# A list schedule that puts an unread product ahead of a ready TensorE operation, by the work over the last clock window

## The chip, the cores and the metric

The kernel runs on one core of one Trainium2 chip. The metric is the device time of that core in microseconds (us), as the median of several executions; lower is better. The core has five engines that the text names as the profile does: PE (TensorE; its weight loads are PEld), DVE (VectorE), ACT (ScalarE), POOL (GpSimd) and SP (SyncE, which here only issues transfers). PE's clock is granted in steps: the profile gives it for every stretch of time as a share of full speed, and here it shows 1.00 or 0.50.

## What is computed

Four layers over one sequence of 512 tokens with 1024 features, each a mixer and then a gated feed-forward block, with a residual sum after both. The four mixers differ. Cut to what matters here:

```python
for i in range(DEPTH):                        # DEPTH = 4
    t = i % 4
    hn = rmsnorm(h, norm_mix[i])
    m = [rwkv7_mix, swa_sink_mix, sgu_chunk_mix, gla_mix][t](hn, ...)
    h = h + m
    h = h + swiglu(rmsnorm(h, norm_ffn[i]), ffn_w_in[i], ffn_w_out[i])
return rmsnorm(h, norm_final)

# rwkv7_mix, one step of its recurrence per token, 16 heads of 64 x 64 states
sa = einsum('bhvk,bhk->bhv', state, kk_t)
state = state * d_t - sa * (kk_t * a_t) + v_t * k_t
y_t = einsum('bhvk,bhk->bhv', state, r_t)
# ... then a norm per head, a gate, and  @ w_o

# swa_sink_mix, 16 query heads on 2 key heads, window of 128 tokens
s = einsum(q, k) / 8, masked;  p = exp(s - max) / (sum + exp(sink - max))
o = einsum(p, v);  return o @ w_o + b_o
```

## The kernel before

**An order that a program writes.** The kernel's code doesn't issue instructions as it runs. Each call on an engine makes an `Op` with its data dependences and an estimated cost (`record`, `price`), and `Program.run` then issues all of them in the order of a list schedule: it keeps an estimated time `now` for each engine, looks at the operations whose inputs are issued within a window of 700, works out for each when it could start (`s`), and takes the one that starts first. All engines run their own queues in that order, so an order that the schedule chose for PE is kept on the chip even where another operation would be ready earlier. Every instruction made in this way carries one line number in the profile, L233 (L234 in the changed kernel); groups are told apart by their tiles.

**Unread products.** The schedule also fills waits of PE. `keep_warm` is called when the operation that was chosen for PE has to wait for its inputs; if the estimated wait is at least `GAP` (450 ns), it issues products of the 128x128 identity with itself (`product`, L448; L478 in the changed kernel) into a PSUM bank that nobody reads, as many as fit until 150 ns before the operation can start. A product is estimated at 224 ns, or 448 ns where the schedule takes the clock for halved. It does so where the columns that it has booked for the tick before (a tick is 10240/3 ns, on a fixed grid; `count` books them) are fewer than `BUSY` = 3350, and it then doubles the estimated cost of any PE operation as well. In the profile one unread product is two records, since a 4-byte product is made in two passes there: `ps<-ident 128*128`.

**The stages that the text speaks of.** All times are of the profiled execution.

- *The RWKV mixer* runs from the start to about 500 us, in four sub-blocks of four heads each. For each: features are prepared (`rwkv_prepare`, whose 512-wide working tiles are called `et`), products of pairs of tokens are made (`rwkv_products`, into `pr`), a triangular matrix is inverted by blocks (`rwkv_inverse`: 16 small products at a time with ACT or DVE between, tiles `mt`, result `iv`), it is applied (`rwkv_direct`), and a chain of eight steps goes over the tokens (`rwkv_chain`): a product gives `x`, ACT copies it into `vu`, a product with `tok` makes the next state, DVE scales it into `st`, and `st` goes into the next step's products. The chain's outer products (`wu` with `iv`, `vu` with `pr`) hang beside it, and `rwkv_out` turns its results (`out`) round with the identity. When the last sub-block's chain ends, the output projection is left: `rwkv_out_proj`, 288 products `et,rk` (moving `et`, stationary `rk`; six of the eight head pairs, 256 columns wide).
- *The attention mixer* (`swa`, about 860 to 1010 us): four query projections for the first key head (`project`: 24 products of 512 columns each, rows `slot,whi` and `slot,wlo`), its scores (`slot 128x256` and `slot 128x128`), a softmax over DVE, ACT and POOL, turning the weights round (`ident,slot`), and the products with the values (`slot 64x512`). The second key head's four projections are independent of the first one's softmax, and so is the output projection's (`whi,slot`, `gemm_tok`) first half of the second one's. I call the two key heads group 1 and group 2.
- Behind 1010 us come the feed-forward block, the other two mixers and their blocks, in which PE hardly waits.

Of the kernel before, what the change touches and what calls it, by code (L numbers as in the profile page):

```python
# [17 lines left out]
P = 128  # L18
# [19 lines left out]
class View:  # L38
# [3 lines left out]
    def __init__(self, buf, dims, p0, lo, steps):  # L42
        self.buf, self.dims, self.p0, self.lo, self.steps = buf, dims, p0, lo, steps
# [146 lines left out]
class Program:  # L190
# [3 lines left out]

    WINDOW, SLACK, SEM = 700, 200.0, 100.0
    FREE, GAP, TAIL, TURN = 4, 450.0, 150.0, 92.0
    TICK, BUSY = 10240 / 3, 3350.0

    def __init__(self, tc):
        self.tc, self.ops, self.last = tc, [], None  # L200
        nc = tc.nc
        self.tensor, self.vector, self.scalar = Engine(self, "PE", nc.tensor), Engine(self, "DVE", nc.vector), Engine(self, "ACT", nc.scalar)
        self.gpsimd, self.sync = Engine(self, "POOL", nc.gpsimd), Engine(self, "SP", nc.sync)
        self.cold, self.warm, self.fills, self.form = 0.0, None, 0, (P, P, 0)

    def pool(self, name, bufs, **kw):
        return Pool(self, name, bufs, kw)
# [80 lines left out]
    def run(self):  # L288
# [9 lines left out]
        now = {e: 0.0 for e in ("PE", "DVE", "ACT", "POOL", "SP", "")}  # L298
        dma, table, work = 0.0, None, {}
# [4 lines left out]
        while order < n:  # L304
            while head < n and ops[head].done:
                head += 1
            new = min(n, head + self.WINDOW)
            for op in ops[limit:new]:
                if op.wait == 0:
                    bisect.insort(avail[op.eng], (op.i, op))  # L310
            limit = max(limit, new)
            best = None
            for e, lst in avail.items():
                cand, floor = None, None
                for i, op in lst:
                    s = max(now[e], op.ready)
                    ok = True
                    for b in op.bufs:
                        if b.held:
                            continue  # L320
                        sl = b.pool.slots[b.name]
                        if not sl.may(b, head) or b.psum and b.span[0] > head and len(sl.free) <= self.FREE and not self.soon(b, head):
                            ok = False
                            break
                        s = max(s, min(sl.free) + self.SEM)
                    if not ok:
                        continue
                    if op.table and op.table != table and not (table and op.table in ALSO.get(table, ())):
                        s += 1300.0
                    if floor is None or s < floor - self.SLACK:  # L330
                        if floor is None or s < floor:
                            floor = s
                        cand = (s, i, op)
                    elif s < floor:
                        floor = s
                    if floor <= now[e]:
                        break
                if cand:

                    if best is None or cand[0] < best[0]:  # L340
                        best = cand + (e,)
            if best is None:
                raise RuntimeError("no instruction can go on at %d of %d: %s" % (order, n, [(e, len(l)) for e, l in avail.items()]))
            s, i, op, e = best
            if e == "PE" and self.warm and op.ready > 0.0:
                now["PE"] = self.keep_warm(now["PE"], s, work)
                if now["PE"] > s:
                    continue
            avail[e].remove((i, op))
            if op.table and op.table != table and not (table and op.table in ALSO.get(table, ())):  # L350
                table = op.table
            cost = op.cost
            if e == "PE":
                if op.form[:2] != self.form[:2]:
                    cost += self.TURN
                elif op.form[0] == 64 and op.form[2] != self.form[2]:
                    cost *= 0.56
                self.form = op.form
                tick = int(s // self.TICK)
                if work.get(tick - 1, 0.0) < self.BUSY:  # L360
                    self.cold += cost
                    cost *= 2
                self.count(work, self.TICK, s, cost, op.columns)
            end = s + cost
            now[e] = end
            fin = end + op.lat
            if op.lat == 2000.0:
                dma = max(dma, s + 1100.0) + max(450.0, op.columns / 360.0)
                fin = dma + 1500.0
            op.end = end  # L370
            for b in op.bufs:
                if not b.held:
                    b.pool.slots[b.name].take(b, head)
            op.call()
            op.done = True
            order += 1
            for b in op.bufs:
                b.till = max(b.till, fin if op.lat == 2000.0 else end + 60.0)
                b.left -= 1
                if b.left == 0:  # L380
                    b.pool.slots[b.name].give(b, head)
            for o in op.outs:
                raw = o.deps[op]
                if o.eng == e and e == "PE" or o.eng == "":
                    t = end
                elif o.eng == e:
                    t = (fin if raw else end) if op.lat != 2000.0 else fin
                else:
                    t = fin if raw else (end + self.SEM if op.lat != 2000.0 else fin)
                o.ready = max(o.ready, t)  # L390
                o.wait -= 1
                if o.wait == 0 and o.i < limit:
                    bisect.insort(avail[o.eng], (o.i, o))
        self.time = max(now.values())

    def keep_warm(self, now, s, work):
# [7 lines left out]
        while True:  # L404
# [7 lines left out]
            t += c  # L412
            now = t

    def count(self, work, span, t, cost, columns):
        n = int(t // span)
        part = min(1.0, ((n + 1) * span - t) / cost)
        work[n] = work.get(n, 0.0) + columns * part
        work[n + 1] = work.get(n + 1, 0.0) + columns * (1.0 - part)
# [1397 lines left out]
```

## Time and profile before

| | us |
|---|---|
| median of 3 runs | 2604.38 |
| the runs | 2601.57, 2606.51, 2604.38 |
| the profiled execution, its own time | 2596.65 |
| its span in the trace | 2595.0 |
| PE busy in it | 2517.9 (97%) |
| unread products | 190 (380 records) |
| granted PE clock, mean | 0.994 |

The profiled execution was 7.7 us faster than the median. The page gives the span and the busy time of each engine; beside it the prediction uses the view of windows (for a stretch of time each engine's busy time and instruction count, the clock granted to PE, the share of the DMA engines), the timeline of one engine (in square brackets the idle time before an instruction, and the operation whose end released it), the groups of instructions by line and form, and the view of waits. The window rows have these columns: from:to in us, length, then busy time and count of PE, PEld, DVE, ACT and POOL, PE clock, DMA share, GB/s.

### The profile page before, as it was taken

The numbers are of one execution on the slowest core, as the hardware profiler recorded it, in microseconds if no ns is written. First come the engines' busy times: TensorE is split into PE (matmuls) and PEld (weight loads), VectorE is DVE, ScalarE is ACT, GpSimd is POOL, SyncE is SP. The second block draws the span as 40 slices with busy tenths as digits, with TensorE's granted clock in tenths as the row PEclk, the third lists the DMA queues.
The fourth block names the chain that finished last, engine by engine and source line by source line (L and its number), as shares of the span: only waits on it lengthen the run. The fifth ranks groups of instructions, "written<-read, shape, count | busy, mean of one in ns | idle before, by whom it ended". The sixth has DMA issues, their size and how long they took to land.

```text
span 2595.0 us, 37573 instructions
## 1 busy us (share of the span) xinstructions
PE 2517.9 (97%) x14378; PEld 2052.6 (79%) x14378; DVE 1802.4 (69%) x2804; ACT 1314.1 (51%) x2156; POOL 377.6 (15%) x521
## 2 busy tenths in 40 slices
PE   9999898999999989999999999999999999999998
PEld 8577777997888756988787888888878777888886
DVE  8685875487778863787776655577868634577868
ACT  4544454465646455656464333565556523565555
POOL 1000111022112232121221000012111000121111
PEclk9999999999999999999999999999999999999999
DMA  3220001489898412898985232389887221489885
GB/s 128 62 75 10 10 4 59 120 195 225 214 225 176 129 49 49 179 211 225 213 218 146 90 98 83 82 216 228 208 213 187 84 81 57 98 219 226 221 199 117
DMA packets 126004, 365.20 MB, mean 141 GB/s; under 512 B 13296, under 2 KB 19952, under 8 KB 125824
## 3 DMA queue, kind: packets, MB, share of 16 engines
q0 software_dynamic: 41472, 138.43, 29.8%
q1 hardware_dynamic: 84352, 224.37, 26.9%
q8 instruction: 113, 1.85, 0.3%
q14 instruction: 67, 0.55, 0.1%
HBM read 358.29 MB, written 2.10 MB: 139 GB/s over the span
## 4 chain that ended last, share of the span: by engine, by line
PE 47%; DMA 5%; issue 5%; DVE 4%; ACT 3%; POOL 0%; SPq 0%; ACTq 0%; POOLq 0%; DVEq 0%
PE ps L233 47%; DMA wraw<-ffn_w_b 3%; DVE slot L233 2%; ACT slot L233 2%; DMA wraw<-ffn_o_a 2%; DVE wlo L233 1%; ACT whi L233 1%; DMA wraw<-ffn_w_a 1%; DVE h L233 0%; POOL wraw L233 0%; DVE mx L233 0%; DMA slot<-slot 0%; SPq L233 0%; DVE left L233 0%; ACT left L233 0%
## 5 line engine op out<-in xcount | busy, mean ns | idle before, releaser
L233 PE MATMUL ps<-whi,slot 128*128 128x512 f32 (+1 forms) x5072 | 1557.7, 384 | 17.8 <-DVE slot L233 9.3
L233 PEld LDWEIGHTS ps<-whi,slot 128*128 128x128 f32 x5072 | 943.7, 188 | 199.5 <-issue 21.4
L233 DVE TENSOR_TENSOR wlo<-wraw,whi 128x1024 fp32r<-128x1024 f32 (+2 forms) x628 | 720.2, 1153 | 398.8 <-ACT whi L233 396.4
L233 ACT CAST whi<-wraw 128x1024 fp32r<-128x1024 f32 (+3 forms) x632 | 625.1, 993 | 732.2 <-PE ps L233 554.7
L233 PE MATMUL ps<-wlo,slot 128*128 128x512 f32 (+1 forms) x2536 | 969.1, 383 | 1.9 <-DVE wlo L233 1.7
L233 PEld LDWEIGHTS ps<-wlo,slot 128*128 128x128 f32 x2536 | 476.9, 188 | 86.1 <-DVE wlo L233 6.2
L233 PE MATMUL ps<-slot,whi 128*128 128x512 f32 (+2 forms) x864 | 275.8, 397 | 0.1
L233 DVE TENSOR_TENSOR slot<-ps,slot 128x512 f32<-128x512 f32 (+2 forms) x287 | 155.0, 566 | 91.0 <-PE ps L233 61.7
L233 PEld LDWEIGHTS ps<-slot,whi 128*128 128x128 f32 (+2 forms) x864 | 157.2, 185 | 48.3 <-issue 6.6
L233 POOL DMA_DIRECT2D wraw<-ffn_w_a x128 | 109.1, 853 | 512.5 <-DVE wlo L233 375.7
L233 PE MATMUL ps<-slot,wlo 128*128 128x512 f32 (+2 forms) x432 | 169.5, 393 | 0.8 <-DVE wlo L233 0.8
L233 POOL DMA_DIRECT2D wraw<-ffn_w_b x64 | 54.7, 859 | 772.7 <-DMA wraw<-ffn_w_b 517.8
L233 DVE TENSOR_TENSOR slot<-left,slot 128x512 fp32r<-128x512 f32 (+1 forms) x214 | 137.5, 661 | 34.3 <-ACT slot L233 28.8
L233 DVE TENSOR_TENSOR h<-h,ps 128x512 f32<-128x512 f32 x192 | 127.1, 683 | 29.8 <-PE ps L233 28.4
L233 ACT CAST slot<-left 128x512 fp32r<-128x512 f32 (+1 forms) x214 | 123.8, 598 | 34.3 <-PE ps L233 26.4
L233 PEld LDWEIGHTS ps<-ident,slot 128*128 128x128 f32 (+1 forms) x676 | 69.2, 141 | 41.9 <-POOL slot L233 14.4
L233 ACT COPY slot<-ps 128x512 f32<-128x512 f32 (+1 forms) x137 | 75.2, 563 | 50.8 <-PE ps L233 49.2
L233 PE MATMUL ps<-ident,slot 128*128 128x128 f32 (+1 forms) x676 | 89.4, 268 | 11.4 <-POOL slot L233 9.0
L233 PEld LDWEIGHTS ps<-slot,wlo 128*128 128x128 f32 (+2 forms) x432 | 79.6, 184 | 21.3 <-issue 3.3
L233 POOL DMA_DIRECT2D wraw<-ffn_o_a x64 | 54.5, 852 | 278.6 <-DVE wlo L233 204.9
L233 ACT COPY left<-ps 128x512 f32<-128x512 f32 x100 | 50.5, 555 | 54.7 <-PE ps L233 54.7
L233 DVE TENSOR_TENSOR slot<-slot 128x512 fp32r<-128x512 f32 (+9 forms) x93 | 62.0, 672 | 15.8 <-ACT slot L233 14.6
(278 smaller groups left out, 2267.3 us busy)
## 6 DMA issues: line engine op xcount, KB each, us to landing
wraw<-ffn_w_a SPq DMA_DIRECT2D x128, 512.0 KB, 6.5
wraw<-ffn_w_a POOLq DMA_DIRECT2D x128, 512.0 KB, 6.1
wraw<-ffn_o_a SPq DMA_DIRECT2D x64, 512.0 KB, 5.0
wraw<-ffn_o_a POOLq DMA_DIRECT2D x64, 512.0 KB, 8.0
wraw<-ffn_w_b SPq DMA_DIRECT2D x64, 384.0 KB, 3.3
wraw<-ffn_w_b POOLq DMA_DIRECT2D x64, 384.0 KB, 6.2
wraw<-ffn_o_b SPq DMA_DIRECT2D x16, 512.0 KB, 4.3
wraw<-ffn_o_b POOLq DMA_DIRECT2D x16, 512.0 KB, 7.7
```

Of the source, the lines that this page charges most:

```text
L233: op = self.add(eng.name, lambda: getattr(eng.target, what)(*map(real, args), **{k: real(a) for k, a in kw.items()}), *self.price(eng.name ...
```

## The change

A method `ahead_of_cold` is called for a PE operation that could start without a wait worth filling. It adds up the columns that PE was given over the last tick's length, up to the end of that operation (a sliding sum over `recent`, which `count` now fills, and not the fixed grid). If the sum is `DENSE` = 3550 or more, the operation is issued, as before, and a flag `armed` is set that is never cleared. If it is less and the flag is set, one unread product is issued ahead of the operation, PE's estimated time moves on by its cost, and the schedule chooses anew among all engines and operations.

```diff
-    TICK, BUSY = 10240 / 3, 3350.0
+    TICK, BUSY, DENSE = 10240 / 3, 3350.0, 3550.0
...
+        self.recent, self.armed = [], False
...
             if e == "PE" and self.warm and op.ready > 0.0:
                 now["PE"] = self.keep_warm(now["PE"], s, work)
-                if now["PE"] > s:
+                if now["PE"] > s or self.ahead_of_cold(now, s, op, work):
                     continue
...
+    def ahead_of_cold(self, now, s, op, work):
+        pool, call, first = self.warm
+        free = pool.slots["ps"].free
+        t, end = max(s, now["PE"]), s + op.cost
+        if not first.done or not free or min(free) + self.SEM > t:
+            return False
+        sum_ = op.columns
+        for b, e, c in reversed(self.recent):
+            if e <= end - self.TICK:
+                break
+            sum_ += c * (e - max(b, end - self.TICK)) / (e - b)
+        if sum_ >= self.DENSE:
+            self.armed = True
+            return False
+        if not self.armed:
+            return False
+        cost = 224.0 if work.get(int(t // self.TICK) - 1, 0.0) >= self.BUSY else 448.0
+        call()
+        self.fills += 1
+        self.form = P, P, 0
+        self.count(work, self.TICK, t, cost, 512.0)
+        now["PE"] = t + cost
+        return True
+
     def count(self, work, span, t, cost, columns):
+        self.recent.append((t, t + cost, columns))
+        if len(self.recent) > 400:
+            del self.recent[:200]
```

Since an added product moves PE's estimated time, it moves the choice of everything behind it, and the order changes in more places than the products stand. There are 280 unread products now, 90 more: 77 net in the RWKV mixer and 13 in the attention mixer. From about 1010 us on PE's order is the same. Three places on PE matter to the prediction.

The first is the last sub-block's inverse (PE, after the wait at 407 us; `mt`, `pr`, `iv` as above, `wu,iv` and `vu,pr` are outer products of chains that run beside it). Before:

```order
L233 MATMUL ps<-wu,iv 64x64 x5
L233 MATMUL ps<-mt 64x64 x16
L233 MATMUL ps<-wu,iv 64x64 x7
L233 MATMUL ps<-ident,mt 64x64 x16
L233 MATMUL ps<-vu,pr 64x64 x3
L233 MATMUL ps<-mt,pr 64x64 x16
L233 MATMUL ps<-vu,pr 64x64
L233 MATMUL ps<-wu,iv 64x64 x2
```

The same place now:

```order
L478 MATMUL ps<-ident 128x128 x2
L234 MATMUL ps<-mt 64x64 x16
L478 MATMUL ps<-ident 128x128 x4
L234 MATMUL ps<-ident,mt 64x64 x16
L478 MATMUL ps<-ident 128x128 x3
L234 MATMUL ps<-mt,pr 64x64 x16
L478 MATMUL ps<-ident 128x128 x4
```

The outer products that stood between the steps have gone behind the inverse, and unread products stand in their place, ahead of each step.

The second is the end of the last chain and the output projection (PE, about 455 to 475 us; `tg,g` is the gate). Before:

```order
L233 MATMUL ps<-vu,tok 128x128 x2
L233 MATMUL ps<-vu,pr 64x64 x4
L233 MATMUL ps<-ident,out 128x128
L233 MATMUL ps<-tg,g_3900 128x256
L233 MATMUL ps<-st_1420,qk 128x128 x2
L233 MATMUL ps<-tg,g_3900 128x256
L233 MATMUL ps<-et,rk 128x256
L233 MATMUL ps<-vu,pr 64x64 x4
L233 MATMUL ps<-et,rk 128x256 x80
L233 MATMUL ps<-ident,out 128x128 x4
L233 MATMUL ps<-et,rk 128x256 x207
```

Now:

```order
L234 MATMUL ps<-vu,tok 128x128 x2
L234 MATMUL ps<-vu,pr 64x64 x4
L234 MATMUL ps<-et,rk 128x256 x5
L234 MATMUL ps<-ident,out 128x128 x4
L234 MATMUL ps<-st_1420,qk 128x128 x2
L234 MATMUL ps<-et,rk 128x256 x9
L234 MATMUL ps<-vu,pr 64x64 x4
L234 MATMUL ps<-et,rk 128x256
L234 MATMUL ps<-ident,out 128x128 x4
L234 MATMUL ps<-tg,g_3985 128x256 x2
L234 MATMUL ps<-et,rk 128x256 x75
L234 MATMUL ps<-ident,out 128x128 x4
```

Of the 288 products `et,rk`, 32 now stand between the steps of the last chain, the first of them right after its first step. The rest, 75 and 181, follow as before.

The third is the wait for group 1's softmax (PE, about 902 to 909 us; with buffer numbers, since the rows read alike without them: `whi_8992` and `wlo_9004` are the weights of one query projection, `ident,slot` is the first turning round). Before:

```order
L233 MATMUL ps_9206<-slot_8970,slot_9166 128x256
L233 MATMUL ps_9218<-slot_8697,whi_8992 128x512
L233 MATMUL ps_9218<-slot_8708,whi_8992 128x512
L233 MATMUL ps_9218<-slot_8697,wlo_9004 128x512
...
L233 MATMUL ps_9218<-slot_8716,whi_8992 128x512
L233 MATMUL ps_9218<-slot_8724,whi_8992 128x512
L233 MATMUL ps_9269<-ident_101,slot_9121 128x128 x2
```

Now:

```order
L234 MATMUL ps_9366<-slot_9124,slot_9320 128x256
L234 MATMUL ps_9379<-slot_8851,whi_9146 128x512
L234 MATMUL ps_9379<-slot_8862,whi_9146 128x512
...
L234 MATMUL ps_9379<-slot_8702,wlo_9158 128x512
L234 MATMUL ps_9425<-slot_8851,whi_9171 128x512
...
L234 MATMUL ps_9425<-slot_8864,wlo_9182 128x512
L234 MATMUL ps_9455<-ident_101,slot_9275 128x128 x2
```

Before, 11 products of one projection stood ahead of the first `ident,slot`; now all 24 of it do, and 9 of the next, 33 in all. The rows at the end of the second group's projections are 38 where they were 62. In group 2, 22 products stand ahead of the first `ident,slot` where 8 did, 25 between the later ones where 14 did, and 49 at the end where 74 did.

## The prediction

> **What bounds the kernel now.** I read the page first: PE is busy for nearly the whole span, and the chain that ended last is mostly PE.
>
> ```profile
> PE 2517.9 (97%) x14378; PEld 2052.6 (79%) x14378; DVE 1802.4 (69%) x2804; ACT 1314.1 (51%) x2156; POOL 377.6 (15%) x521
> PE 47%; DMA 5%; issue 5%; DVE 4%; ACT 3%; POOL 0%; SPq 0%; ACTq 0%; POOLq 0%; DVEq 0%
> ```
>
> So a product that is added where PE has no wait costs its whole duration, and a gain can come from two things alone: waits of PE that useful products fill, and time at half clock. The second thing I looked for in the view of windows, cut on the clock's own edges. Leaving out the start and the last microseconds there are six windows at half clock, here with the window ahead of each of the first five:
>
> ```profile
> 282.11:285.53 3.42, 1.43 (x17) 0.39 (x12) 1.65 (x3) 0.00 (x0) 2.95 (x9) 1.00 0.19 40
> 285.53:288.94 3.41, 3.27 (x37) 2.56 (x37) 3.41 (x4) 0.58 (x1) 2.24 (x4) 0.50 0.11 41
> 445.95:449.37 3.42, 1.55 (x14) 1.32 (x15) 1.65 (x5) 1.73 (x4) 1.16 (x6) 1.00 0.01 2
> 449.37:452.78 3.41, 3.37 (x17) 2.67 (x17) 0.77 (x2) 0.36 (x1) 1.80 (x9) 0.50 0.00 0
> 906.75:910.17 3.42, 0.92 (x5) 0.67 (x6) 3.38 (x11) 2.63 (x12) 1.72 (x3) 1.00 0.00 0
> 910.17:913.58 3.41, 3.41 (x8) 1.07 (x6) 3.38 (x9) 2.17 (x8) 1.60 (x3) 0.50 0.00 0
> 964.78:968.19 3.41, 1.01 (x5) 0.49 (x3) 3.41 (x12) 2.60 (x14) 0.00 (x0) 1.00 0.02 7
> 968.19:971.60 3.41, 1.10 (x4) 0.94 (x5) 3.38 (x9) 3.41 (x16) 1.77 (x4) 0.50 0.00 0
> 971.60:975.02 3.42, 3.17 (x10) 1.11 (x8) 3.42 (x10) 3.42 (x15) 0.61 (x2) 0.50 0.00 0
> 1097.90:1101.31 3.41, 3.41 (x14) 3.24 (x13) 1.56 (x3) 1.28 (x4) 0.00 (x0) 0.50 0.74 230
> ```
>
> The window ahead of a halved one has PE busy for 0.92 to 1.55 us of 3.4. The halved window itself costs at most half of PE's busy time in it: 1.6, 1.7, 1.7, 0.6, 1.6 and 1.7 us. About 9 us of 2595 is thus the most that the clock can give back.
>
> The two attention groups, ahead of and behind their softmax:
>
> ```profile
> 902.10:909.10 7.00, 2.77 (x12) 1.97 (x11) 6.96 (x23) 6.06 (x29) 0.65 (x2) 1.00 0.48 182
> 909.10:938.10 29.00, 27.79 (x107) 13.17 (x107) 13.09 (x32) 20.33 (x68) 16.90 (x16) 0.94 0.15 42
> 938.10:952.40 14.30, 14.30 (x63) 11.57 (x62) 7.02 (x10) 4.46 (x9) 3.52 (x2) 1.00 0.28 67
> 963.70:970.50 6.80, 2.09 (x9) 1.40 (x8) 6.77 (x20) 4.91 (x25) 0.67 (x2) 0.83 0.13 48
> 970.50:998.20 27.70, 26.14 (x99) 12.11 (x99) 10.21 (x31) 19.93 (x70) 13.77 (x15) 0.92 0.00 1
> ```
>
> PE waits for the softmax (over 4 us in each first row), is close to full while it turns the weights round, and then works off independent projection products with no wait at all (14.30 of 14.30). Products that the third stretch holds could run in the first.
>
> The RWKV stage, by the pieces that the added products fall into:
>
> ```profile
> 190.00:225.00 35.00, 34.89 (x547) 27.79 (x545) 11.29 (x15) 9.77 (x20) 3.58 (x5) 1.00 0.03 10
> 289.00:314.00 25.00, 20.68 (x426) 17.31 (x426) 18.46 (x34) 10.35 (x24) 0.00 (x0) 1.00 0.01 3
> 331.00:361.00 30.00, 29.51 (x553) 23.35 (x551) 16.74 (x29) 14.01 (x30) 5.82 (x19) 1.00 0.01 2
> 361.00:408.50 47.50, 45.22 (x469) 36.76 (x469) 41.15 (x98) 26.75 (x60) 9.32 (x36) 1.00 0.19 63
> 408.50:432.90 24.40, 21.74 (x533) 19.42 (x533) 13.31 (x21) 8.83 (x19) 4.54 (x17) 1.00 0.10 28
> 432.90:460.30 27.40, 21.91 (x195) 18.11 (x195) 9.70 (x24) 10.52 (x28) 3.17 (x16) 0.94 0.04 11
> 460.30:495.50 35.20, 35.20 (x303) 34.90 (x302) 14.94 (x30) 7.36 (x14) 5.61 (x18) 1.00 0.48 151
> ```
>
> Length less PE's busy time is PE's wait: 0.1, 4.3, 0.5, 2.3, 2.7, 5.5 and 0 us. All but the last run at a clock of 1.00 or nearly. So most of the added products stand where the clock isn't short.
>
> **The change part by part.** *An unread product's price.* The PE timeline has a run of them behind the output projection, and one ahead of the last inverse's first step:
>
> ```profile
> 495.49 4.74 PE L448 MATMUL ps<-ident 128*128 128x128 f32 x41
> 407.10 1.05 PE L448 MATMUL ps<-ident 128*128 128x128 f32 x8
> 408.53 1.15 PE L233 MATMUL ps<-ident,mt 64*64 64x64 f32 x32 [0.37 <-DVE mt L233]
> ```
>
> 41 records are 21 products (two each, one unrecorded): 4.74/21 = 0.226 us each. The 77 of the RWKV stage are 17.4 us if nothing hides them, the 13 of attention 2.9.
>
> *RWKV, the added products.* Nine stand at 195 to 212 us, in a stretch with 0.1 us of wait: 9 x 0.226 = +2.0, and nothing hides them. Fifteen stand at 289 to 310 us, in 4.3 us of wait. There PE, ACT and DVE hand one inverse to each other; a product put ahead of a ready step delays that step and all behind it, so the wait helps only where the schedule mistimed the readiness. Bounds 0 (all in the wait) and 3.4; I take a third hidden, +2.3, since the order puts them ahead of ready steps. Ten at 340 to 360: 2.3, at most 0.5 hidden, +1.8. Seven new ones at 372 to 388, net of two removed, and 16 more ahead of the `ident,mt` at 408.5 stand in a wait that DVE ends: 0 for themselves, and +5.2 if DVE's work came early enough not to cover them. Twenty at 408 to 433 (4.5 us; the first order piece): the outer products that they replace have gone into the next stretch, and 2.7 us of wait lies here. Bounds 0 and 4.5; I take +1.0, near the lower end, as DVE and ACT steps between the products set this inverse's pace and the outer products had filled the same holes.
>
> *ACT's order.* The exponentials of the last sub-block (its table load ahead) now come one chain step later on ACT, and that sub-block's inverse hangs on them through DVE:
>
> ```profile
> 369.48 1.28 ACT L233 ACT_TABLE_LOAD   x1
> 370.77 0.63 ACT L233 ACTIVATE et<-ew 128x512 f32<-128x512 f32 x1
> 434.98 0.68 PE L233 MATMUL ps<-st,ident 128*128 128x128 f32 x4 [1.15 <-DVE st L233]
> ```
>
> A chain step is about 3 us. DVE is busy 41.15 of 47.5 us behind it, so DVE has 6 us of slack for it but spread out: bounds 0 and +3.0, taken +2.2, near the upper end since the wait at 408.5 is DVE's.
>
> *The output projection.* 32 of its products go into the last chain's waits:
>
> ```profile
> L233 PE MATMUL ps<-et,rk 128*128 128x256 f32 x288 | 34.7, 281 | 0.0
> 447.33 0.71 PE L233 MATMUL ps<-vu,tok 128*128 128x128 f32 x4 [1.45 <-ACT vu L233]
> 471.12 24.53 PE L233 MATMUL ps<-et,rk 128*128 128x256 f32 x207
> ```
>
> The group is busy 34.7 us for 288, 0.120 each, and 32 are 3.8 us less at the end, where PE has no wait (24.53 us for the last 207, to 495.65). They fit the 5.5 us of waits in the last chain. The 19 outer products of the first order piece that moved into it cost 0.7 (1.15 us for 32 of their size, 0.036 each), and the halved window at 449 (up to 1.7) gives back 0.6, since the chain there waits for ACT and DVE more than for PE. Together -3.7; bounds -6 and 0 (if they delay the chain by as much).
>
> RWKV: 2.0 + 2.3 + 1.8 + 0 + 1.0 + 2.2 - 3.7 = **+5.6 us**.
>
> *Attention, group 1.* The wait and the pace of the products moved into it:
>
> ```profile
> 909.12 1.01 PE L233 MATMUL ps<-ident,slot 128*128 128x128 f32 x4 [4.25 <-POOL slot L233]
> 970.50 0.69 PE L233 MATMUL ps<-ident,slot 128*128 128x128 f32 x2 [4.71 <-POOL slot L233]
> L233 PE MATMUL ps<-slot,whi 128*128 128x512 f32 x41 | 12.8, 392 | 0.0
> L233 PE MATMUL ps<-slot,wlo 128*128 128x512 f32 x21 | 8.2, 390 | 0.0
> ```
>
> The durations in these groups overlap; the stretch has 62 such products in 14.30 us, 0.23 each. 22 more ahead of the first `ident,slot` are 5.1 us in a wait of 4.25, so the turn starts about 0.8 late, but those 5.1 us are gone from the end; the halved window behind the wait (1.7) gives back about 1, and four unread products are 0.3 after a short stall ahead of the scores. -5.1 + 0.8 - 1.0 + 0.3 = **-5.0**; bounds -6 and -1.
>
> *Group 2.* 25 products leave the end: 14 go into the wait of 4.71 (3.2 us, all of it fits) and 11 between the later turns, where 1.6 us of wait lies (taken as 0.8 gained). Halved windows at 968 and 972 give back 1.5 of their 2.2. Nine unread products are 2.0, half of them in a stall. -3.2 - 0.8 - 1.5 + 1.0 = -4.5, taken with group 1 as **-9.5**; bounds -12 and -2.
>
> *The sum:* 5.6 - 9.5 = -3.9 us on a span of 2595.0, so 2591.1. That execution was 7.7 under the median of 2604.4; no row says what a slower one pays, so I carry the difference over: 2604.4 - 3.9 = **2600.5**. Its own range is 2597 to 2604.
>
> **What a page says against it.** The rows at 282 and 445 us show the clock halved behind windows that PE was busy for 1.43 and 1.55 us, with no single wait of 3 us in them. The Trainium skill ("TensorE: Matmul & The Clock Gate", Part 1, What's actually happening) puts the fall to half clock after at least one idle window of some 3.4 us, on a free-running grid. By its idle window the added products in the RWKV stage would be bought for nothing, and only attention's waits could cool the clock; the trace speaks against the idle window, and for the length of the window. By its free-running grid, other executions would show the halved windows elsewhere; one profiled execution can't show that.
>
> **The rivals.**
>
> *The added products are paid in full.* If PE, ACT and DVE hand the inverse on in one serial chain, each product ahead of a step delays it: 2.0 + 3.4 + 2.3 + 4.5 + 2.2 - 3.7 = 10.7 in the RWKV stage, and with -5 in attention the sum is +5.7, with the 16 ahead of `ident,mt` up to +9. That is 2610 to 2613, 2612. For it speaks that waits there are short and each names one ACT or DVE result; against it, 4.3, 2.7 and 5.5 us of wait in those stretches. It decides from an RWKV end that is over 10 us late.
>
> *The softmax bounds attention.* If ACT (6.06 of 7.00 us, then 20.33 of 29) and POOL set the pace of the turns, and the projection's products had been filling holes that now stay empty, attention gains 2 instead of 9.5: +3.6, 2608. Against it, PE is busy 27.79 of 29.00.
>
> *More is hidden and more cooled than this execution shows.* If the added products lie in waits (RWKV 2.0 + 1.8 + 1.0 + 1.0 - 5.0 = +0.8), attention gains 11 and an ordinary execution has some of its extra 7.7 us from halved windows that the change takes away, the sum is -10 or more: 2594 or lower.
>
> *The change doesn't do what it says.* No added product stands near 285, 449, 906, 968 or 1098 us, since the schedule doesn't expect those waits: where moved work doesn't fill them, the halved windows stay. Then 3 us of the gain are missing: -0.9, 2603.5.
>
> **How the numbers follow.** About 0.2% (5.2 us) is what a measurement tells from no change: faster is below 2599.2, slower above 2609.6. The forecast has a chance of 0.36, and 0.17 of it lies below 2599.2; the hidden case 0.27; paid in full 0.20; the softmax 0.12, a third of it above 2609.6 with some fills paid; nothing done 0.05, all of it no change. Faster: 0.27 + 0.17 = 0.44. Slower: 0.20 + 0.04 = 0.24. No change: 0.32. The range takes in both neighbours, down to 2590 and up to 2612.
>
> **What would show it.** The windows at 910, 968 and 972 at full clock and the wait ahead of the first `ident,slot` under 1 us: attention as forecast, the stretch from the scores to the feed-forward block about 9 us shorter. The end of `et,rk` 3 to 8 us behind 495.65: RWKV as forecast; over 10 behind it: paid in full. Wrong from the ground up would be a changed end behind 1010 us, where PE's order is the same, or unread products at 195 us that cost nothing.

## The result, and the profile after

The changed kernel takes 2621.43 us in the median of 4 runs (2617.23 to 2623.36), the kernel before 2602.98 in 4 runs beside it (2598.9 to 2606.51). The ratio is 1.0077, with a 95% interval of 1.0059 to 1.0095: 0.8% slower, where no change to a small gain was forecast (2600.5 us, and at most 2612). The profiled execution has a span of 2619.5 us against 2595.0, so 24.5 more.

The page's busy times and the chain that ended last:

```profile
PE 2559.7 (98%) x14558; PEld 2085.0 (80%) x14558; DVE 1803.8 (69%) x2804; ACT 1314.0 (50%) x2156; POOL 378.0 (14%) x521
PE 48%; DMA 6%; DVE 5%; issue 3%; ACT 3%; POOL 1%; SPq 0%; ACTq 0%; POOLq 0%; DVEq 0%
```

PE is busy 41.8 us longer, with 180 records (90 products) more. At the price that the prediction used, 90 x 0.226 = 20 us of busy time were to be expected. The page alone thus says that either a product costs more or other work takes longer; the mean granted clock is 0.994 in both traces, so it isn't the clock's mean.

To see where the time went I paired the instructions of the two traces (the n-th PE instruction with given tiles and shape in the one with the n-th in the other, unread products left out) and took the median difference of their starts, the shift, by stretches of the kernel before. One anchor of it is in the view by tile, whose columns are the duration's minimum, median and maximum in ns and the first and last start. Before:

```profile
L233 PE MATMUL ps<-twa,wa x8: 589/590/694, 221.5 to 222.9; 64*128 64x512 f32 x8
L233 PE MATMUL ps<-et,rk x288: 276/280/472, 460.3 to 495.4; 128*128 128x256 f32 x144
```

After:

```profile
L234 PE MATMUL ps<-twa,wa x8: 589/589/693, 230.0 to 231.4; 64*128 64x512 f32 x8
L234 PE MATMUL ps<-et,rk x288: 277/281/471, 470.5 to 524.1; 128*128 128x256 f32 x144
```

The output projection of the RWKV mixer ends 28.7 us later (524.1 against 495.4), where 5.6 was forecast. The attention mixer takes 5.5 us of it back (the shift is 29.9 ahead of it and 24.4 behind), where 9.5 was forecast, and behind it the shift ends at 24.5. By stretch, with the first experiment beside it (the same order, with ahead_of_cold's 59 products not issued and the 31 that `keep_warm` adds left in); 46 of the 59 stand in the RWKV mixer:

| stretch of before, us | forecast | changed kernel | without the 59 (e1) | difference |
|---|---|---|---|---|
| to 190 | 0 | +3.6 | +1.1 | 2.5 |
| 190 to 225 | +2.0 | +4.9 | +0.8 | 4.1 |
| 285 to 325 | +2.3 | +8.7 | +1.3 | 7.4 |
| 325 to 361 | +1.8 | +4.4 | +0.8 | 3.6 |
| 361 to 408 | +2.2 | +4.0 | +5.3 | -1.3 |
| 408 to 435 | +1.0 | +8.9 | +5.2 | 3.7 |
| 435 to 500 | -3.7 | -5.9 | -5.7 | -0.2 |
| RWKV mixer | +5.6 | +28.7 | +8.8 | 19.9 |
| attention | -9.5 | -5.5 | -6.9 | 1.4 |

**What a single product does.** The place at 205 us, where PE has no wait, shows it. (The rows count records: one unread product is two.) PE's timeline before:

```profile
200.85 2.23 PE L233 MATMUL ps<-slot 64*64 64x64 f32 x64
203.00 0.50 PE L233 MATMUL ps<-whi,slot 128*128 128x512 f32 x1
```

and after:

```profile
204.94 1.52 PE L234 MATMUL ps<-slot 64*64 64x64 f32 x40
206.39 0.49 PE L478 MATMUL ps<-ident 128*128 128x128 f32 x2
206.81 0.92 PE L234 MATMUL ps<-slot 64*64 64x64 f32 x24
207.66 0.73 PE L234 MATMUL ps<-whi,slot 128*128 128x512 f32 x2
```

The same 64 records took 2.15 us to the next instruction (200.85 to 203.00) and now take 2.72 (204.94 to 207.66) with one unread product in their middle: it costs 0.57 us, not 0.226. The last inverse shows how such products fill and overfill the waits between the steps. Before, two steps of it came 1.9 us apart, each behind a short wait:

```profile
426.17 1.15 PE L233 MATMUL ps<-ident,mt 64*64 64x64 f32 x32 [0.35 <-DVE mt L233]
...
428.04 1.15 PE L233 MATMUL ps<-mt,pr 64*64 64x64 f32 x32 [0.24 <-ACT mt L233]
```

And after:

```profile
453.69 1.80 PE L478 MATMUL ps<-ident 128*128 128x128 f32 x8
455.42 1.15 PE L234 MATMUL ps<-ident,mt 64*64 64x64 f32 x32
456.50 1.58 PE L478 MATMUL ps<-ident 128*128 128x128 f32 x6
458.01 1.15 PE L234 MATMUL ps<-mt,pr 64*64 64x64 f32 x32
459.09 2.13 PE L478 MATMUL ps<-ident 128*128 128x128 f32 x8
461.14 1.08 PE L234 MATMUL ps<-mt 64*64 64x64 f32 x29
```

None of these rows has a wait in brackets any more: PE goes from products to a step and back without idle time, and each step comes 2.6 to 3.1 us behind the one before it.

**The clock.** These are the windows, cut on the clock's edges, around two stretches that are halved after. The first was full in the trace before; in the second, one window was halved (285.53 to 288.94):

```profile
155.57:158.98 3.41, 1.68 (x9) 0.89 (x7) 3.41 (x8) 1.05 (x2) 0.00 (x0) 1.00 0.44 153
158.98:162.39 3.41, 3.41 (x11) 1.19 (x9) 3.38 (x9) 1.63 (x3) 0.00 (x0) 0.50 0.00 1
162.39:165.81 3.42, 3.42 (x16) 2.90 (x17) 3.28 (x6) 0.00 (x0) 0.00 (x0) 0.50 0.02 5
292.10:295.51 3.41, 1.36 (x30) 1.00 (x31) 2.59 (x3) 0.00 (x0) 3.23 (x7) 1.00 0.11 37
295.51:298.93 3.42, 3.42 (x38) 2.63 (x34) 3.42 (x6) 2.64 (x5) 0.80 (x2) 0.50 0.00 0
298.93:302.34 3.41, 3.41 (x31) 2.84 (x32) 1.91 (x5) 0.41 (x2) 0.00 (x0) 0.50 0.03 7
302.34:305.75 3.41, 3.41 (x46) 3.25 (x42) 2.40 (x5) 0.30 (x1) 0.00 (x0) 0.50 0.00 0
```

The products didn't keep the clock: three windows in a row are halved at 295 to 306, behind a window with 1.36 us of PE work, and PE is busy in them from end to end. In all there are eight halved windows between the start and the last microseconds; there were six. e1, without the 59 products, has eight as well.

**Attention.** The PE timeline from group 1's scores to the first turn:

```profile
928.40 2.13 PE L478 MATMUL ps<-ident 128*128 128x128 f32 x8 [0.66 <-DVE slot L234]
930.45 4.79 PE L234 MATMUL ps<-slot 64*128 64x128 f32 x24
...
942.56 0.39 PE L234 MATMUL ps<-slot,wlo 128*128 128x512 f32 x1
942.79 0.38 PE L234 MATMUL ps<-ident,slot 128*128 128x128 f32 x2
```

The moved projection products have closed the wait of 4.25 us: `ident,slot` follows without a gap, as forecast. But the four added products hold the last scores back by 2 us, and the clock is halved there (930 to 934 us), so that 24 records take 4.79 us where they took 3.68.

### The profile page after: what moved, and what is told of

Same layout as the page of the kernel before. It is cut to its first block, busy times and chain, and to the rows that moved or that the text cites. A ratio compares the mean times of both kernels' runs of the same rounds, so it can differ in the third digit from the quotient of the medians.

```text
span 2619.5 us, 37934 instructions
## 1 busy us (share of the span) xinstructions
PE 2559.7 (98%) x14558; PEld 2085.0 (80%) x14558; DVE 1803.8 (69%) x2804; ACT 1314.0 (50%) x2156; POOL 378.0 (14%) x521
## 4 chain that ended last, share of the span: by engine, by line
PE 48%; DMA 6%; DVE 5%; issue 3%; ACT 3%; POOL 1%; SPq 0%; ACTq 0%; POOLq 0%; DVEq 0%
PE ps L234 47%; DMA wraw<-ffn_o_a 3%; DMA wraw<-ffn_w_b 2%; DVE slot L234 2%; ACT slot L234 2%; DVE wlo L234 1%; ACT whi L234 1%; DVE mx L234 1%; POOL wraw L234 0%; DVE h L234 0%; DMA wraw<-ffn_w_a 0%; PE ps L478 0%; DVE left L234 0%; ACT left L234 0%; DMA slot<-slot 0%
## 5 line engine op out<-in xcount | busy, mean ns | idle before, releaser
L234 DVE TENSOR_TENSOR h<-h,ps 128x512 f32<-128x512 f32 x192 | 127.2, 683 | 29.9 <-PE ps L234 28.6
L478 PE MATMUL ps<-ident 128*128 128x128 f32 x560 | 89.5, 296 | 4.0 <-POOL ident L234 1.4
L478 PEld LDWEIGHTS ps<-ident 128*128 128x128 f32 x560 | 75.7, 198 | 14.3 <-PE ps L478 5.5
```

Of the source, the lines that this page charges most:

```text
L234: op = self.add(eng.name, lambda: getattr(eng.target, what)(*map(real, args), **{k: real(a) for k, a in kw.items()}), *self.price(eng.name ...
L478: self.nc.tensor.target.matmul(self.ps.tile_pool.tile([P, S], F32, name="ps")[:, :P], self.ident.real(), self.ident.real(), start=True, st ...
```

## The experiments

Shifts are worked out as above, against the profiled execution of the kernel before. Where a run was timed, its ratio to the kernel before (beside it on the same chip) has its 95% interval.

**e1: the changed order without ahead_of_cold's products.** Of the 90 added products, 59 come from the new method and 31 more from `keep_warm`, which finds other waits in the changed plan. Here the 59 are booked but not issued:

```diff
         cost = 224.0 if work.get(int(t // self.TICK) - 1, 0.0) >= self.BUSY else 448.0
-        call()
         self.fills += 1
```

> The changed kernel's schedule with the 59 products of ahead_of_cold booked in the plan but not issued, so every other instruction stands in the changed order; 221 unread products are left (31 more than before, all put by keep_warm). If the added products themselves cost the time (dear price theory: 46 of them in the RWKV mixer at about 0.5 us each among 64-row products), the RWKV mixer ends about 23 us earlier than in the changed kernel and the whole is near 2600. If the moved order costs it (order theory), the time stays above 2614. If the halved windows at 159 and 295 us cost it (clock theory), those windows are back at full clock only if they came from the products, and the time lies between, about 2610.

2598.94 us, ratio 0.9998 (0.9988 to 1.0008). The changed order, with `keep_warm`'s 31 products in it, costs nothing on the whole; the whole loss hangs on the 59. The RWKV mixer ends 8.8 us later than before instead of 28.7, so its 46 products cost 19.9 us, 0.43 each (with one halved window more at 159 us and one more at 295 than e1 has there). Two halved windows at 289 us and one at 159 are there without them.

**e2: the same products, the order of before.** The 59 are issued ahead of the same operations, and the plan doesn't know of them (`EXTRA` is the list of places and counts):

```diff
+            for _ in range(EXTRA.get(op.i, 0)):
+                self.warm[1]()
             for b in op.bufs:
```

> The kernel before, its order untouched, with the same 59 products issued ahead of the same 59 places but not booked in the plan. Dear price theory: about 46 x 0.5 = 23 us more in the RWKV mixer and up to 4 in attention, 2622 to 2630. Order theory: at most 46 x 0.226 = 10 us more and part of that hidden, 2606 to 2613.

2629.18 us, ratio 1.0109 (1.0091 to 1.0127). The RWKV mixer is 21.6 us longer (0.47 for each of 46), the attention mixer 8.9, which nothing moved takes back (eight windows are halved there, against three before). The order theory falls.

**p1, p2, p3: the price by itself.** Twenty more unread products in the kernel before, with the same edit as e2: one at a time between 64x64 products of opposite halves of the array (p1), in one run ahead of a product of the output projection (p2), and one at a time, seven of its products apart (p3). Each of the p runs is one traced execution.

> The kernel before with 20 more unread products, one at a time, each between two 64x64 products that use opposite halves of the array, at 190 to 210 us where PE has no wait. Flat price theory (0.226 us, as in a run): the stretch behind is 4.5 us later. Dear price theory (0.4 to 0.6 us between small products): 8 to 12 us later.

> The kernel before with 20 more unread products in one run, ahead of one product of the output projection at about 485 us where PE has no wait. Both theories: 4.5 us later from there on.

> The kernel before with 20 more unread products, one at a time, seven products of the output projection apart (128 rows, 256 columns each). If the price is dear because a single product stands alone: 8 to 12 us later. If it is dear only where it stands between products of opposite halves: 4.5 to 6 us later.

From right ahead of the places to behind them the shift rises by 11.6 us in p1, 4.5 in p2 and 4.4 in p3: 0.58, 0.22 and 0.22 us for one product. A product that stands alone isn't dear; one among 64-row products is. The timeline of p1 shows one of the places:

```profile
196.54 0.68 PE L236 MATMUL ps<-slot,pa 64*64 64x64 f32 x16
197.06 0.28 PE L236 MATMUL ps<-ident,slot 64*64 64x64 f32 x2
197.26 0.49 PE L453 MATMUL ps<-ident 128*128 128x128 f32 x2
197.68 0.79 PE L236 MATMUL ps<-ident,slot 64*64 64x64 f32 x18
```

and the weight loads beside it:

```profile
197.00 0.19 PEld L236 LDWEIGHTS ps<-ident,slot 64*64 64x64 f32 x2
197.26 0.30 PEld L453 LDWEIGHTS ps<-ident 128*128 128x128 f32 x2
197.68 0.54 PEld L236 LDWEIGHTS ps<-ident,slot 64*64 64x64 f32 x16
```

Among the small products, the loads run ahead of the products that use them (197.00 against 197.06). At the change to 128 rows and back each load starts only when its product does (197.26 and 197.26, 197.68 and 197.68). In p3, where all neighbours have 128 rows, the load starts 0.11 us ahead of its product:

```profile
470.22 0.38 PE L453 MATMUL ps<-ident 128*128 128x128 f32 x2
470.11 0.30 PEld L453 LDWEIGHTS ps<-ident 128*128 128x128 f32 x2
```

The rows thus place the cost at the two changes of size. That the late loads make it, and don't merely come with it, isn't shown.

**p6: ten pairs.** Two in a row at ten of p1's places.

> The kernel before with 20 more unread products at ten of the twenty places of p1, two in a row at each. If the dear part is paid once for each change from 64-row products to a 128-row one and back (0.58 - 0.22 = 0.36), 10 x (0.36 + 2 x 0.22) = 8.0 us later. If each product there costs 0.58 whatever stands beside it, 11.6.

The shift rises by 8.0 us: 0.36 for a change of size and back, paid once, and 0.22 for each product. The same two prices give e2's RWKV mixer: 44 of its 46 products stand at 32 places among 64-row products, and 32 x 0.36 + 46 x 0.22 is about 21.6 us, as measured.

**p4: half the array.** One at a time at p1's places, of 64 rows and columns:

```diff
+            i = self.ident.real()[:64, :64]
+            self.nc.tensor.target.matmul(self.ps.tile_pool.tile([P, S], F32, name="ps")[:64, :64], i, i, start=True, stop=True)
```

> The kernel before with 20 more unread products at the twenty places of p1, each of 64 rows and 64 columns instead of 128 (the identity's first quarter with itself), so the array's size isn't changed. If the change of size is what costs, 20 x 0.06 = about 1.2 us later; if it is the break in the alternation of the two halves, 20 x 0.2 or more, 4 us or later.

1.8 us for twenty, 0.09 each. It is the change of size that costs, not the break in the alternation of halves (rows and columns were changed together, so which of them counts stays open).

**e3: attention alone.** The RWKV mixer's instructions stand as before; 13 products are added.

```diff
-                if now["PE"] > s or self.ahead_of_cold(now, s, op, work):
+                if now["PE"] > s or op.i >= 6639 and self.ahead_of_cold(now, s, op, work):
```

> ahead_of_cold is asked only for operations from the attention mixer on, so the RWKV mixer is that of before, instruction for instruction, and 13 products are added. All theories: the end of the RWKV mixer as before, the attention mixer about 5.5 us shorter, 2597 to 2598. If attention's gain in the changed kernel was a matter of the clock's phase after a shifted start, 2601 to 2604 instead.

2594.77 us, ratio 0.9981 (0.997 to 0.9992): faster than both kernels. The mixer is 4.9 us shorter. (The traced execution was the fastest of its 12.)

**e6: from the last chain on.** As e3, with 3200 in place of 6639.

> ahead_of_cold is asked only for operations from number 3200 on (the last sub-block's chain, the output projection, and all behind it). No product of it stands between 64x64 products of the inverses then; keep_warm puts 18 more in the RWKV mixer than before, and 40 or so products of the output projection stand between the steps of the last chain. Dear price theory: RWKV mixer 2 to 4 us shorter than before, attention 5.5 shorter, 2591 to 2594. If the moved order behind the last inverse is bad in itself, 2597 to 2602.

2594.39 us, ratio 0.9979 (0.997 to 0.9989). The RWKV mixer is 3.0 us shorter, as the spread output projection was to give, but attention only 1.0, with five halved windows in it. The 18 more products in the RWKV mixer are ahead_of_cold's and not `keep_warm`'s, as was expected: e15, which doesn't issue them, has the count of before there.

**e8: the plan's threshold.** `BUSY` at 3000, and e3's condition.

> The plan takes the clock for halved behind a tick with fewer than 3000 columns instead of 3350 (the trace's ticks have at most 2752 ahead of a halved one), and ahead_of_cold is asked from the attention mixer on. The plan's own halved time falls from 38.9 us (attention alone) to 30.4. If the plan's wrong idea of the clock spoils the order in the RWKV mixer, 2588 to 2593; if not, like attention alone, 2594 to 2597.

2601.16 us, ratio 1.0007 (0.9996 to 1.0018). A threshold nearer to the trace's columns doesn't make a better order by itself. In the traced execution, the slowest of its 12, the RWKV mixer is 9.1 us longer, with four halved windows in it where there were two; why wasn't followed up.

**e10: the last inverse bare.** As e1, and `keep_warm`'s 19 products planned at 420 to 440 us not issued:

```diff
-            call()
+            if not 420e3 <= t < 440e3:
+                call()
```

> As e1 (the changed order, ahead_of_cold's 59 products not issued), and besides the 19 products that keep_warm planned at 420 to 440 us between the steps of the last inverse are not issued. If those overflow the short waits they stand in (each change of array size about 0.4 us), the stretch that was at 408 to 433 us in the kernel before is 2 to 4 us shorter than in e1, its shift of +12 at 420 to 430 us falls to about +9, the late start that ACT's order makes. If the waits of that inverse are DVE's and hide them, it stays at +12 to +13.

2597.8 us, ratio 0.9997 (0.9984 to 1.0009). The shift goes from 9.7 at 410 us to 13.5 at 435 (e1: 9.4 to 14.5), so only 1.4 us are won, and two windows at 429 us are halved that were full. What those 19 cost and what they gave can't be told apart here.

**e13: the same for planned waits under 2 us, in e3.** `keep_warm` doesn't issue ahead of 64x64 products there (19 fewer).

> e3 (ahead_of_cold asked from the attention mixer on) and besides the 19 products that keep_warm puts ahead of 64x64 products into planned waits under 2 us are not issued, the plan untouched. If such products cost more than the wait they stand in already in the kernel before, the RWKV mixer is 2 to 5 us shorter than in e3, 2590 to 2593; if they are hidden, or hold the clock where it counts, 2594 to 2598.

2597.0 us, ratio 0.9992 (0.9981 to 1.0004). Not better than e3 in the median; removing the kernel's own products among small ones gains nothing that these runs show.

**e14 and e15: attention's and the late order without the products.** e3 and e6 with `call()` left out of ahead_of_cold, as in e1.

> As e3 (ahead_of_cold asked from the attention mixer on), with its 13 products booked in the plan but not issued, so that the attention mixer has the changed order alone. In the runs so far the mixer became 5.4, 4.9 and 1.0 us shorter with the 13 products (changed kernel, e3, e6) and 6.9 and 9.8 shorter with the order alone (e1, e10). If the products take back what they cost, 7 to 10 us shorter here, 2589 to 2592. If they hold the clock and pay for themselves, no better than e3, 2594 to 2596.

> As e6 (ahead_of_cold asked from operation 3200 on) with its products booked but not issued. Products in the wrong place theory: RWKV mixer 3 to 4 us shorter than before by the spread output projection, attention 7 to 10 shorter, 2586 to 2590. If the unread products were what made e6 faster, 2594 or more.

e14: 2592.54 us, ratio 0.9967 (0.9954 to 0.9981). e15: 2589.32 us, ratio 0.9955 (0.9939 to 0.9971). In both, PE has as many records as in the kernel before, 14378, and 190 unread products; they differ from it by order alone. e15 has the lowest median of all versions, 1.2% under the changed kernel by the two ratios; its interval overlaps e14's. Its projection ends 2.7 us earlier:

```profile
L234 PE MATMUL ps<-et,rk x288: 276/280/468, 449.2 to 492.7; 128*128 128x256 f32 x144
```

Attention's change over the traces: -6.9, -9.8, -7.1, -7.0 and -11.2 with the changed order and no products (e1, e10, e14, e15, e16); -5.5, -4.9, -1.0, -3.9 and -0.7 with the 13 products (the changed kernel, e3, e6, e8, e13; e6 has 14). No value of the one list lies in the other's range. The five p runs, whose instructions there are those of before, changed by -1.0 to +1.5, which is the noise of such a value. Nor did the products save halved windows: attention has 3, 1, 4, 5 and 1 of them in the first list, 2, 3, 5, 4 and 6 in the second, and 3 in the kernel before.

**e16: the exponentials pinned.** As e1, with the plan told that three copies of the chain follow the last exponential:

```diff
+        for i in (3264, 3286, 3292):
+            ops[i].deps[ops[2852]] = False
```

> As e1 (the changed order, 59 products not issued), with one thing pinned in the plan: the four exponentials of the last sub-block come on ACT ahead of the chain's next three copies, as in the kernel before. If ACT's order is what makes the last inverse start late, the shift of 9.4 us that e1 shows at 405 to 415 us falls by about 5, to 4 or 5. If the late start is that of the products ahead of it, it stays at 9.

One execution, 2594.03 us. The shift at 405 to 415 us is 10.9, not 4 or 5, but the test doesn't decide by this number: three windows at 371 to 381 us were halved in this execution, and the exponentials still stood behind other copies that wait for PE.

## Why the prediction was wrong

Between the forecast and the trace lie 28.4 us (-3.9 against +24.5), 23.1 of them in the RWKV mixer and 4.0 in attention.

*The unread product's price.* This is the step that failed. The prediction took 0.226 us from a run of products behind the output projection, and called 77 x 0.226 = 17.4 us the most that the RWKV stage could pay. p2 shows that the price is right for a run. But 44 of ahead_of_cold's 46 products there stand ahead of 64-row products, one to four at a time, and there one costs 0.58 and a second 0.22 more (p1, p6). The 46 cost 19.9 us in place (e1) and 21.6 with the old order (e2). The bound was therefore no bound: it came from a run of equal products, and not from a row with the same neighbours. The order piece quoted ahead of the prediction, `ident` between `mt` products, already showed the neighbours, and the trace before had a hint of the price:

```profile
409.60 0.33 PE L233 MATMUL ps<-ident,qk 128*128 128x128 f32 x1
409.86 1.15 PE L233 MATMUL ps<-mt,pr 64*64 64x64 f32 x32
```

This single 128-row record between 64-row ones takes 0.26 us to the next instruction, where a record in the run takes 0.12 (4.74/41). The nine at 195 us, for which "nothing hides them" was right, cost 4.1 us and not 2.0.

*What hides them.* A third of the fifteen at 289 us was taken as hidden. They cost 7.4 us in 4.3 us of former wait, 0.49 each, one more halved window included; with the old order and one halved window, as before, they cost 8.2 (e2). Fifteen products at 13 places are 13 x 0.36 + 15 x 0.22 = 8.0 by the prices above: none of it was hidden. The rival "paid in full" had this mechanism; its sum of 10.7 us had the same wrong price.

*ACT's order.* Taken as +2.2; the stretch that holds it is 5.3 us later in e1. The rows that carry it there, first one of the kernel before, then ACT's timeline of e1:

```profile
369.10 0.36 ACT L233 COPY vu<-ps 64x256 f32<-64x256 f32 x1
374.25 0.37 ACT L234 COPY vu<-ps 64x256 f32<-64x256 f32 x1 [0.51 <-PE ps L234]
...
377.99 0.37 ACT L234 COPY vu<-ps 64x256 f32<-64x256 f32 x1 [0.47 <-PE ps L234]
378.37 1.28 ACT L234 ACT_TABLE_LOAD   x1
379.67 2.19 ACT L234 ACTIVATE et<-ew 128x512 f32<-128x512 f32 x4
```

The table load came right behind the copy at 369.10, and now stands behind two such copies that wait for PE: it comes at 378.37 against 369.48, 8.9 later where the stage was 4 late. What follows shows that this is what the inverse waits for, in e1:

```profile
416.69 1.05 DVE L234 TENSOR_TENSOR mt<-et,mk 128x512 f32<-128x512 f32 x1
417.88 1.15 PE L234 MATMUL ps<-ident,mt 64*64 64x64 f32 x32
```

PE's first step starts 0.14 us behind the end of DVE's `mt`, as it does in the kernel before (408.38, 408.53) and in the changed one. From the end of the last exponential to that step it takes 35.0 us before (373.58 to 408.53) and in e2, e3, e6 and e14, and 36.0 in e1, e10 and the changed kernel (381.86 to 417.88 in e1). DVE's work behind the exponentials thus had no slack, where the prediction gave it 6 us, spread out: of the 9.4 us that the step is late in e1, 8.3 are the exponentials' lateness. e16 fits as well (384.11 to 419.44, 35.3). The products that fill PE's wait ahead of that step end as it can start, and cost nothing, as forecast.

*The last inverse and the output projection.* The inverse was taken at +1.0; it is +5.2 in e1 and +8.9 with the products. With nothing in place of the outer products it is still +3.8, with two halved windows (e10); what makes it longer stays open. The output projection was right in kind, and its stretch gave more than the forecast 3.7: 5.7 to 5.9 us in e1 and the changed kernel, 6.3 in e6 and e15; the halved window at 449 us, worth up to 1.7, is gone in all four. In e6 and e15 the stretch ahead of it is 1.2 to 3.5 us longer, and e15 lost 1.8 to halved windows at 287 us, so that the mixer as a whole is 3.0 and 2.7 us shorter.

*Attention.* The wait of 4.25 us is gone and the order is worth 7 to 11 us, which holds the forecast of 9.5. The mis-sized term is the 13 products: +1.3 net was taken, and they cost 1.4 (e1 against the changed kernel), 2.2 (e14 against e3) and 6 us (e15 against e6), with the clock's part in it.

*The clock.* That the added products stand where the clock isn't short was right, and the gain of 3 us from windows made full didn't come: both attention groups have a halved window again, at 930 and 988 us, now ahead of the former wait and not behind it.

*The free-running grid.* It was held that other executions would show halved windows elsewhere if the grid runs freely (the Trainium skill, "TensorE: Matmul & The Clock Gate", Part 1, What's actually happening). The runs agree. e3 and e14 have the same instructions up to attention; the rows of 280 to 300 us, e3's first:

```profile
280.00:300.00 20.00, 15.71 (x288) 11.89 (x288) 18.16 (x29) 3.84 (x8) 6.83 (x16) 1.00 0.06 16
```

e14's:

```profile
280.00:300.00 20.00, 17.31 (x258) 14.20 (x255) 15.19 (x24) 4.32 (x9) 7.49 (x18) 0.74 0.06 15
```

The clock is full in the one and 0.74 in the other, and e14's RWKV mixer ends 3.7 us later than e3's, 3 of them from here. Repeated runs of one kernel spread by some 10 us (e3: 2589.2 to 2599.4); how much of that is the clock isn't shown.

## What to carry to other kernels

A filler instruction has to be priced between the neighbours that it will stand between, and a bound taken from a run of equal ones is none: ask what it stops from overlapping. If a filler must stand among small products, make it small too: here one of 64 rows cost 0.09 us and one of 128 cost 0.58 (whether the small one holds the clock wasn't tried). When a scheduler both adds instructions and moves others, run the moved order without the additions; here the gain was in the order from the last chain on, and what was added made 19.9 of the 28.7 us that the RWKV mixer lost.

## What the runs showed of the hardware

- Changing PE from 64-row products to a 128-row one and back costs 0.36 us at a clock of 1.00 (p1, p6); at both edges the weight load starts with its product and not ahead of it (p1). The Trainium skill ("TensorE: Matmul & The Clock Gate", Part 3, The mechanism) has weight loads overlap products in flight only where the row group differs. That no load runs ahead at the change would agree with it, but in p3 loads of 128-row products run 0.11 us ahead among products that all use 128 rows, so the rule in these words doesn't hold here.
- The same instructions find the clock halved in different places: behind 285, 449 and 736 us in some executions and not in others. Three halved windows at 286 us cost e14 2.8 us against the trace before, which has one there. At 736 us e14 loses 5.5 us, but 2.9 of these are a longer wait of PE for DVE (4.06 us against 1.21), with two halved windows behind it.
